# A third plain pair, a pool for the token sums, shifted weight parts and an in-place PV sum in a two-block transformer kernel

## The chip, the cores and the metric

The kernel runs on one core of a Trainium2 chip. The metric is the device time of one launch in microseconds. The kernel before takes 3598.26 us, the median of three runs (3597.29 to 3599.67).

## What is computed

Two transformer blocks of two layers each run one after the other on 512 tokens of width 1024, all in float32. The change lies mostly in the second block; each of its layers is

```python
h = rms_norm_2(x, norm1_g)
...
mix = jnp.concatenate([o_a.astype(x.dtype), o_b, o_c], axis=-1) @ w_out
x = x + mix
x = x + conv_glu_ffn(rms_norm_2(x, norm2_g), w_up, conv_w, conv_b, w_down)
```

with a causal convolution of width 3 over the tokens in the feed-forward:

```python
h = x @ w_up                       # 1024 x 5632
a, b = h[..., :D_FF], h[..., D_FF:]
...
return (jax.nn.silu(conv) * b) @ w_down
```

The first block has two attentions in parallel (eight heads of kind "a" and four of kind "b", over 768 keys in its first layer), an adaptive modulation computed from `c` and a gated branch sum; one part of the change touches the "a" heads there.

## The kernel before, in words

Every large product is made exact enough by splitting both operands into two parts: `hi` is the operand rounded to the short matmul format (`F32R`), `lo` the rest. A product is then three matmuls, hi by hi, hi by lo, lo by hi. All of them go through `mm` (L189). ACT makes the hi part of a weight tile by a cast (L291), DVE the lo part by a subtraction (L292); `whi` and `wlo` have two buffers each.

**The feed-forward of the second block** is `ffn2`. The 5632 columns of `w_up` come in 22 tiles of 256 columns: 11 pairs, one tile for the convolution branch and one for the gate branch. The first `NPLAIN` = 2 pairs are done by `plain`: 96 matmuls of 256 columns for a tile. The other 9 pairs are done by `strassen`, which needs only seven block products in place of eight: 7 x 12 = 84 matmuls of 256 columns. It takes sums of weight blocks (`strassen_weights`: POOL makes s3, s1, s2, s4 at L1818 to L1821, ACT and DVE split them into `shi` and `slo` at L1825 and L1826) and sums of token blocks. The seventh product, of s4, is owed: it is issued by `settle` in the course of the next tile, and s4 has two places in `shi` that are used in turn (`odd`).

The token sums are made once a layer, by the generator `steps` in `strassen_setup`, one of four steps after each plain tile: POOL multiplies x by the norm's `r` (L1768), ACT scales by the gain (L1769), POOL forms four differences (L1773 to L1776), ACT and DVE split the results into `ha`, `hb` and `ht` (L1778 to L1786). The plain tiles don't wait for `r`: they take x times the gain (`dhi`, `dlo`, `shi`, `slo` and `g`, L1756 and L1757, which use buffers that the block products and the down products need only later), and `r` is applied to their result (L1899, L1901).

The down products (`down`) run in chunks of two pairs: four of them, each 24 matmuls of 512 columns, are put behind the tiles of the next chunk, one behind each tile. Chunk 1 are the pairs 2 and 3.

All of these buffers but the weight parts and the scratch `tmp` are in the pool `fp`, which is opened when `ffn2` begins. The mixer's last product is cut in two halves of tokens; DVE adds each piece of it into x (L1727), ACT squares the sum (L367), the squares are summed (L369) and give `r` (L423 to L426).

**The "a" heads of the first block.** In `back` (L938 to L943) the upper 64 rows of a head's product with V are copied by ACT to a buffer `small`, and DVE adds them to the lower 64 rows. There are three such buffers, which also serve the sums of the modulation (`small<-raw,cc`, L592): these sums, their transposes (`n<-ident,small`) and the gate's product (`n<-h,whi`) are woven in between the heads.

The order on each engine is set when the program is built, by a scheduler that places an instruction where its inputs and its buffer are expected to be ready. A buffer that comes free earlier thus moves instructions.

## Time and profile before

| | |
|---|---|
| median of three runs | 3598.26 us |
| the profiled execution, its own time | 3594.57 us |
| its span, first to last instruction | 3592.8 us |
| mean granted TensorE clock | 0.979 |
| PE busy | 3394.7 us, 94% |
| DVE busy | 2526.9 us, 70% |
| ACT busy | 1497.2 us, 42% |
| POOL busy | 1053.7 us, 29% |

PE is TensorE, DVE is VectorE, ACT is ScalarE, POOL is GpSimd. The feed-forward of the second block runs from about 2533 to 2900 us in its first layer and from about 3203 to 3593 us in its second. The clock is a share of 2.4 GHz; 0.5 is the lower level of 1.2 GHz. A busy PE counts overlapping matmuls once, so its pace is read from the starts of the matmuls in the timeline.

### The profile page before, as it was taken

Reading aid. Unit: us, or ns where it says so; the run is one execution under the profiler, and the core shown is the slowest. Engines: PE = TensorE matmul, PEld = TensorE weight load, DVE = VectorE, ACT = ScalarE, POOL = GpSimd, SP = SyncE. Lnnn points to the kernel's source line nnn. Section 1 sums busy time; section 2 is a strip of 40 time slices with the busy share of each in tenths; the row PEclk is TensorE's granted clock in tenths of the full one; section 3 lists DMA queues with packets and bytes.
Section 4 is the critical chain, followed back from the end, with each engine's and each line's share of the span. In section 5 each row is a group of like instructions: output and inputs, shape, how many; then the busy total and the mean of one; then the engine's idle time right before and its main releaser. Section 6 shows DMA issues by size and latency. Waiting matters only on the chain.

```text
span 3592.8 us, 51031 instructions
## 1 busy us (share of the span) xinstructions
PE 3394.7 (94%) x19782; PEld 2936.4 (82%) x19782; DVE 2526.9 (70%) x4138; ACT 1497.2 (42%) x2415; POOL 1053.7 (29%) x968
## 2 busy tenths in 40 slices
PE   7998989999999999999999999979899998998998
PEld 5887878888888887877888887867899976778998
DVE  5558775558787765655767656797887769869775
ACT  4234545342222234355543334425544433455444
POOL 2232322320000012312231001563654326527441
PEclk9999999999999999999999999989999999999999
DMA  6376533412334423663444233443133342612331
GB/s 223 115 232 181 165 106 114 151 60 94 96 123 135 129 81 106 220 168 102 118 143 135 93 115 105 132 147 100 59 112 104 102 142 88 179 52 85 102 104 65
DMA packets 358609, 438.79 MB, mean 122 GB/s; under 512 B 41342, under 2 KB 310288, under 8 KB 358368
## 3 DMA queue, kind: packets, MB, share of 16 engines
q1 hardware_dynamic: 327648, 345.48, 32.0%
q0 software_dynamic: 19200, 71.17, 5.7%
q10 hardware_dynamic: 11520, 18.89, 1.6%
q8 instruction: 156, 2.56, 0.3%
q14 instruction: 85, 0.70, 0.1%
HBM read 363.78 MB, written 71.70 MB: 121 GB/s over the span
## 4 chain that ended last, share of the span: by engine, by line
PE 61%; DVE 10%; issue 3%; POOL 2%; ACT 2%; DMA 2%; ACTq 0%; SPq 0%; DVEq 0%; POOLq 0%
PE d L189 34%; PE s L189 18%; PE n L189 4%; DVE wlo L292 1%; PE o L189 1%; DVE sc L1424 1%; PE g L189 1%; DVE m L1423 1%; PE d L202 1%; PE b L202 1%; ACT whi L291 1%; DVE wlo L1813 0%; DVE slo L1826 0%; DVE hl L399 0%; DVE tmp L1355 0%
## 5 line engine op out<-in xcount | busy, mean ns | idle before, releaser
L189 PE MATMUL s<-h,whi 128*128 128x256 f32 (+3 forms) x2176 | 527.4, 335 | 11.1 <-ACT whi L291 6.4
L291 ACT CAST whi<-raw 128x2048 fp32r<-128x2048 f32 (+2 forms) x195 | 311.5, 1597 | 463.2 <-PE s L189 234.0
L292 DVE TENSOR_TENSOR wlo<-raw,whi 128x2048 fp32r<-128x2048 f32 (+3 forms) x179 | 357.5, 1997 | 180.1 <-ACT whi L291 179.2
L189 PE MATMUL d<-h,whi 128*128 128x512 f32 (+2 forms) x1456 | 443.7, 387 | 16.2 <-DVE h L1302 6.1
L189 PEld LDWEIGHTS s<-h,whi 128*128 128x128 f32 (+1 forms) x2176 | 373.9, 192 | 54.3 <-ACT whi L291 6.7
L189 PE MATMUL s<-h,wlo 128*128 128x256 f32 (+3 forms) x1088 | 360.9, 333 | 2.3 <-DVE wlo L292 2.3
L189 PEld LDWEIGHTS d<-h,whi 128*128 128x128 f32 (+1 forms) x1456 | 270.3, 191 | 76.2 <-DVE h L1302 8.3
L189 PE MATMUL d<-h,wlo 128*128 128x512 f32 (+2 forms) x728 | 278.3, 386 | 1.6 <-DVE wlo L292 1.6
L189 PEld LDWEIGHTS s<-h,wlo 128*128 128x128 f32 (+1 forms) x1088 | 207.8, 191 | 22.6 <-DVE wlo L292 3.0
L189 PE MATMUL n<-h,whi 128*128 128x512 f32 (+1 forms) x768 | 214.0, 363 | 4.4 <-ACT tmp L1006 2.8
L189 PE MATMUL d<-g,dhi 128*128 128x512 f32 x640 | 197.8, 391 | 0.0
L369 POOL TENSOR_TENSOR small<-small,tmp 128x256 f32<-128x256 f32 x36 | 32.8, 910 | 541.2 <-ACT tmp L367 510.8
L648 DVE TENSOR_REDUCE sm<-s 128x1 f32<-128x768 f32 (+1 forms) x160 | 134.2, 844 | 69.1 <-PE s L189 67.8
L650 ACT ACTIVATE e<-s,sm 128x768 f32<-128x768 f32 (+1 forms) x160 | 130.7, 818 | 116.7 <-DVE sm L648 96.0
L189 PE MATMUL s<-ku,ku 96*128 96x512 f32 (+3 forms) x720 | 154.6, 346 | 20.3 <-ACT e L650 14.4
L189 PE MATMUL d<-g,whi 128*128 128x256 f32 (+1 forms) x688 | 166.7, 337 | 6.4 <-DVE x L1101 2.3
L189 PE MATMUL s<-g,whi 128*128 128x256 f32 (+1 forms) x688 | 167.6, 335 | 0.0
L189 PEld LDWEIGHTS d<-h,wlo 128*128 128x128 f32 (+1 forms) x728 | 139.1, 191 | 29.5 <-issue 2.4
L189 PE MATMUL d<-ht,shi 128*128 128x256 f32 x864 | 161.4, 287 | 0.0
L189 PEld LDWEIGHTS s<-ku,ku 96*128 96x128 f32 (+1 forms) x720 | 120.8, 192 | 45.7 <-ACT e L650 20.4
L189 PEld LDWEIGHTS n<-h,whi 128*128 128x128 f32 x768 | 135.1, 192 | 23.8 <-ACT tmp L1006 3.7
L189 PE MATMUL d<-whi,h 128*128 128x256 f32 x768 | 148.8, 289 | 0.0
(553 smaller groups left out, 9000.9 us busy)
## 6 DMA issues: line engine op xcount, KB each, us to landing
raw<-in__w_up SPq DMA_DIRECT2D x88, 1024.0 KB, 5.1
raw<-in__w_in SPq DMA_DIRECT2D x53, 1024.0 KB, 5.4
araw<-in__w_ada SPq DMA_DIRECT2D x28, 1024.0 KB, 5.3
raw<-in__w_down SPq DMA_DIRECT2D x40, 512.0 KB, 3.5
draw<-in__w_down SPq DMA_DIRECT2D x40, 512.0 KB, 3.5
raw<-in__w_out SPq DMA_DIRECT2D x16, 1024.0 KB, 5.1
raw<-in__w_ada SPq DMA_DIRECT2D x15, 1024.0 KB, 9.7
U<-qd SPq DMA_DIRECT2D x32, 256.0 KB, 4.3
```

The source lines that it names most:

```text
L189: self.last = self.nc.tensor.matmul(*a, **k)
L202: return self.nc.tensor.transpose(*a, **k)
L291: self.nc.scalar.copy(hi, raw[:, 0:n])
L292: (self.nc.gpsimd if self.wpool else self.nc.vector).tensor_tensor(lo, raw[:, 0:n], hi.bitcast(F32), op=OP.subtract)
L369: (self.nc.gpsimd if e else self.nc.vector).tensor_tensor(acc[e], acc[e], sq, op=OP.add)
L648: nc.vector.tensor_reduce(m[:, 0:1], s, axis=AX.X, op=OP.max, negate=True)
L650: nc.scalar.activation(e, s, AF.Exp, bias=m[:, 0:1], accum_out=m[:, 1:2])
L1423: nc.vector.max(m8[t], sc[t])
L1424: nc.vector.match_replace(sc[t], m8[t], sc[t], TAKEN)
```

## The change

- `NPLAIN` goes from 2 to 3: the pair 2 is done by plain products as well, 192 matmuls in place of 168.
- Chunk 1's four down products all go behind the two tiles of pair 3, two behind each; `settle` follows each.
- `ha`, `hb` and `ht` get a pool of their own, `fq`, opened after `fp`. `fp` becomes smaller by them.
- In the first half of each step (k < 4), one DVE instruction multiplies x by the gain and by `r`, in place of POOL's multiply and ACT's scale.
- The parts of the weights of block products and of their sums lie one behind the other, 56 floats (224 bytes) into a slightly larger buffer. s4 has one place; `odd` is gone.
- In `back`, ACT copies one half of the product straight into `oa`, and DVE adds the other half in place; the buffer `small` isn't used.
- The last norm's small tiles get a tag of their own.

```diff
-NPLAIN = 2
+NPLAIN = 3
+SHIFT = 56
...
                 b = (hh % 2) * 64
-                tmp = self.small()[0:64]
-                nc.scalar.copy(tmp, po[64:128, 0:256])
-                nc.vector.tensor_tensor(oa[hh // 2][b:b + 64, q], po[0:64, 0:256], tmp, op=OP.add)
+                o = oa[hh // 2][b:b + 64, q]
+                nc.scalar.copy(o, po[64 - b:128 - b, 0:256])
+                nc.vector.tensor_tensor(o, po[b:b + 64, 0:256], o, op=OP.add)
                 return
...
-        self.shi = self.t(fp, [P, 5, 512], F32R, "shi", 1)
-        self.slo = self.t(fp, [P, 5, 512], F32R, "slo", 1)
+        self.shi, self.slo = [self.t(fp, [P, 2176], F32R, tag, 1)[:, SHIFT:SHIFT + 2048].rearrange("p (i n) -> p i n", i=4)
+                              for tag in ("shi", "slo")]
...
-        ha = [[self.t(fp, [P, H], F32R, "ha", 8) for _ in range(2)] for _ in range(4)]
-        hb = [[self.t(fp, [P, S], F32R, "hb", 8) for _ in range(2)] for _ in range(4)]
+        ha = [[self.t(fq, [P, H], F32R, "ha", 8) for _ in range(2)] for _ in range(4)]
+        hb = [[self.t(fq, [P, S], F32R, "hb", 8) for _ in range(2)] for _ in range(4)]
...
-        self.sT = [[self.t(fp, [P, 4, H], F32R, "ht", 8) for _ in range(2)] for _ in range(4)]
+        self.sT = [[self.t(fq, [P, 4, H], F32R, "ht", 8) for _ in range(2)] for _ in range(4)]
...
                     u.append(self.tmp(S))
+                    if k < 4:
+                        nc.vector.scalar_tensor_tensor(u[-1], x[k], gain[:, k:k + 1], r, op0=OP.mult, op1=OP.mult)
+                        continue
                     nc.gpsimd.tensor_tensor(u[-1], x[k], r, op=OP.mult)
                     nc.scalar.activation(u[-1], u[-1], AF.Copy, scale=gain[:, k:k + 1])
...
-        hi, lo = [self.t(self.wp, [P, 2048], F32R, tag, 2).rearrange("p (k n) -> p k n", k=KD) for tag in ("whi", "wlo")]
...
+        hi, lo = [self.t(self.wp, [P, 2048], F32R, tag, 2)[:, SHIFT:SHIFT + 1536].rearrange("p (i n) -> p i n", i=3)
+                  for tag in ("whi", "wlo")]
...
-        for d, v in ((slice(3, 5), flat(self.sraw)), (slice(1, 2), s2), (slice(2 - 2 * o, 3 - 2 * o), s4)):
+        for d, v in ((slice(2, 4), flat(self.sraw)), (slice(0, 1), s2), (slice(1, 2), s4)):
...
-            steps = self.strassen_setup(x, r, col["norm2"], fp)
+            steps = self.strassen_setup(x, r, col["norm2"], fp, self.pool(es, "fq", self.other()))
...
-                per = len(todo) // (2 * npair)
...
+                for i, t in enumerate(tiles):
+                    up(*t)
+                    if t[0] >= NPLAIN:
+                        for _ in range(len(todo) // (len(tiles) - i)):
```

In the built program the pool `fp` of the kernel before reaches over the place of the mixer's last operands (`mix`), which PE reads until its last matmul there; with `ha`, `hb` and `ht` outside it, `fp` ends below that place. So the order of instructions moves at the start of `ffn2`. First ACT, in the first layer of block 2, around the last pieces that the mixer adds into x. The squares are L367 before (L368 in the change), the plain parts L1756 (L1757). Before:

```order
L367 ACTIVATE tmp_22038<-x_21093 128x256
L367 ACTIVATE tmp_22041<-x_21094 128x256
L367 ACTIVATE tmp_22044<-x_21095 128x256
L367 ACTIVATE tmp_22123<-x_21090 128x256
L367 ACTIVATE tmp_22126<-x_21091 128x256
L367 ACTIVATE tmp_22129<-x_21092 128x256
L367 ACTIVATE tmp_22132<-x_21093 128x256
L367 ACTIVATE tmp_22135<-x_21094 128x256
L291 CAST whi_22369<-raw_22367 128x2048
L423 ACT_TABLE_LOAD
L423 ACTIVATE r_19222<-n_22048,sel_71 128x256
L1756 ACTIVATE dhi_22163<-x_21088,cols_2788_17499 128x256
L1756 ACTIVATE dhi_22163<-x_21089,cols_2788_17499 128x256
```

and in the change:

```order
L368 ACTIVATE small_21985<-x_21048 128x256
L1757 ACTIVATE dhi_22126<-x_21048,cols_2748_17459 128x256
L368 ACTIVATE small_21986<-x_21049 128x256
L1757 ACTIVATE dhi_22126<-x_21049,cols_2748_17459 128x256
L368 ACTIVATE tmp_21989<-x_21050 128x256
L1757 ACTIVATE dhi_22126<-x_21050,cols_2748_17459 128x256
L368 ACTIVATE tmp_21992<-x_21051 128x256
L1757 ACTIVATE dhi_22126<-x_21051,cols_2748_17459 128x256
L368 ACTIVATE tmp_21995<-x_21052 128x256
L1757 ACTIVATE shi_22124<-x_21052,cols_2748_17459 128x256
L368 ACTIVATE tmp_21998<-x_21053 128x256
```

Before, the first plain part `dhi` stands behind all squares of both token halves, a weight cast and the norm's first root. In the change each part stands right behind the square of the same x.

Next DVE, in the first layer, where the norm's `r` is ready and the token sums begin. L1899, L1888 and L1889 (L1905, L1894 and L1895 in the change) are the convolution of a plain tile, L1779 and L1782 (L1783 and L1786) the low parts of the sums. Before:

```order
L1899 TENSOR_TENSOR tmp_22329<-d_22231,r_19222 128x512
L1888 SCALAR_TENSOR_TENSOR ya_22331<-tmp_22329,colsw_2791_17509,ya_22331 128x511
L1899 TENSOR_TENSOR tmp_22337<-d_22232,r_19222 128x512
L1889 SCALAR_TENSOR_TENSOR ya_22331<-tmp_22329,colsw_2791_17509,ya_22331 128x510
L292 TENSOR_TENSOR wlo_22506<-raw_22503,whi_22505 128x2048
L1888 SCALAR_TENSOR_TENSOR ya_22339<-tmp_22337,colsw_2791_17509,ya_22339 128x511
L1779 TENSOR_TENSOR ha_22202<-tmp_22345,ha_22201 128x256
L1889 SCALAR_TENSOR_TENSOR ya_22339<-tmp_22337,colsw_2791_17509,ya_22339 128x510
L1779 TENSOR_TENSOR hb_22210<-tmp_22348,hb_22209 128x512
```

and in the change:

```order
L1905 TENSOR_TENSOR tmp_22292<-d_22194,r_19182 128x512
L1905 TENSOR_TENSOR tmp_22300<-d_22195,r_19182 128x512
L1770 SCALAR_TENSOR_TENSOR tmp_22308<-x_21048,cols_2748_17459,r_19182 128x512
L1894 SCALAR_TENSOR_TENSOR ya_22294<-tmp_22292,colsw_2751_17469,ya_22294 128x511
L1894 SCALAR_TENSOR_TENSOR ya_22302<-tmp_22300,colsw_2751_17469,ya_22302 128x511
L1895 SCALAR_TENSOR_TENSOR ya_22294<-tmp_22292,colsw_2751_17469,ya_22294 128x510
L1783 TENSOR_TENSOR ha_22165<-tmp_22308,ha_22164 128x256
L1895 SCALAR_TENSOR_TENSOR ya_22302<-tmp_22300,colsw_2751_17469,ya_22302 128x510
L1783 TENSOR_TENSOR hb_22173<-tmp_22310,hb_22172 128x512
L1770 SCALAR_TENSOR_TENSOR tmp_22443<-x_21049,cols_2748_17459,r_19182 128x512
```

The row L1770 is new: x times the gain times `r`, in place of POOL's L1768 for the same x.

Last PE, in the first layer of block 1, where the last "b" heads and the first "a" heads meet. `s<-tmp,sel` sums the squares of the "b" heads, `s<-ku,heads` spreads their norm, `s<-ku,ku` are scores, `n<-ident,small` the modulation's transposes, `n<-h,whi` the gate's product. Before:

```order
L189 MATMUL s_4035<-ku_4020,heads_75 128x512
L189 MATMUL s_4035<-ku_4020,heads_75 128x256
L189 MATMUL s_4047<-ku_3677,ku_3678 128x512 x3
L189 MATMUL s_4047<-ku_3677,ku_3678 128x256 x3
L189 MATMUL s_4060<-ku_3677,ku_3678 128x512 x3
L189 MATMUL s_4060<-ku_3677,ku_3678 128x256 x3
L202 MATMUL n_4162<-ident,small_4144 128x128 x2
L202 MATMUL n_4162<-ident,small_4145 128x128 x2
L189 MATMUL s_4116<-ku_3677,ku_3678 128x512 x3
L189 MATMUL s_4116<-ku_3677,ku_3678 128x256 x3
L189 MATMUL n_4170<-h_433,whi_3854 128x512
L189 MATMUL n_4170<-h_434,whi_3854 128x512
```

and in the change:

```order
L190 MATMUL s_3998<-tmp_3999,sel_71 8x512
L190 MATMUL s_3998<-tmp_3999,sel_71 8x256
L190 MATMUL s_3998<-tmp_4003,sel_71 8x512
L190 MATMUL s_3998<-tmp_4003,sel_71 8x256
L190 MATMUL s_3998<-tmp_4007,sel_71 8x512
L190 MATMUL s_3998<-tmp_4007,sel_71 8x256
L190 MATMUL n_4168<-h_433,whi_3854 128x512
L190 MATMUL n_4168<-h_434,whi_3854 128x512
L190 MATMUL n_4168<-h_433,wlo_3855 128x512
L190 MATMUL n_4168<-h_435,whi_3854 128x512
L190 MATMUL n_4168<-h_436,whi_3854 128x512
L190 MATMUL n_4168<-h_435,wlo_3855 128x512
```

Before, the gate's product comes after the spread norm and three groups of scores. In the change its 24 matmuls of 512 columns, and then 24 of 256, stand ahead of `s<-ku,heads`, among the last products of the heads with V.

## Rows read from the trace of the kernel before

**Rows 1.** The page: span, and busy time of each engine

```profile
span 3592.8 us, 51031 instructions
...
PE 3394.7 (94%) x19782; PEld 2936.4 (82%) x19782; DVE 2526.9 (70%) x4138; ACT 1497.2 (42%) x2415; POOL 1053.7 (29%) x968
```

**Rows 2.** Timeline of PE in the steady part: start us, us, instruction, xcount

```profile
2702.67 0.63 PE L189 MATMUL d<-g,dhi 128*128 128x512 f32 x2
...
2708.14 0.40 PE L189 MATMUL d<-hb,shi 128*128 128x256 f32 x2
...
2712.45 0.40 PE L189 MATMUL d<-ht,shi 128*128 128x256 f32 x2
```

**Rows 3.** Busy time by stretch, layer 0 of ffn2; count of instructions behind each

```profile
core 0: us, PE busy (x) PEld busy (x) DVE busy (x) ACT busy (x) POOL busy (x), PEclk, DMA share, GB/s
2525.00:2540.00 15.00, 11.08 (x80) 10.43 (x79) 11.48 (x27) 11.62 (x25) 3.20 (x4) 0.93 0.38 123
2560.00:2580.00 20.00, 20.00 (x169) 20.00 (x168) 19.19 (x17) 10.04 (x16) 19.92 (x15) 1.00 0.26 85
2580.00:2600.00 20.00, 12.02 (x82) 11.32 (x81) 19.93 (x17) 12.38 (x22) 17.23 (x12) 0.81 0.09 26
2600.00:2620.00 20.00, 18.53 (x120) 17.19 (x119) 19.81 (x22) 8.25 (x16) 14.16 (x10) 0.93 0.35 114
2700.00:2800.00 100.00, 100.00 (x690) 93.56 (x689) 79.21 (x110) 47.57 (x71) 46.49 (x27) 1.00 0.33 103
```

**Rows 4.** Busy time by stretch, layer 1 of ffn2

```profile
3200.00:3220.00 20.00, 13.95 (x86) 12.96 (x85) 14.82 (x29) 12.48 (x26) 8.06 (x5) 0.83 0.25 79
3260.00:3280.00 20.00, 11.85 (x58) 10.52 (x59) 20.00 (x17) 10.24 (x18) 20.00 (x14) 0.74 0.10 28
```

**Rows 5.** What PE waited for from 2520 to 2640: us, times, longest

```profile
PE d L189 <- ACT ha L1778: 4.4, 1, 4.4
PE d L189 <- ACT dhi L1756: 3.8, 1, 3.8
```

**Rows 6.** What PE waited for from 3200 to 3310

```profile
PE d L189 <- DVE ha L1779: 4.5, 2, 2.4
PE n L189 <- DVE small L369: 4.4, 1, 4.4
```

**Rows 7.** Timeline of POOL: its first work on the token sums, layer 0

```profile
2550.54 2.56 POOL L1768 TENSOR_TENSOR tmp<-x,r 128x512 f32<-128x512 f32 x2 [4.16 <-DVE r L426]
```

**Rows 8.** Timeline of PE: the first block product, layer 0

```profile
2586.20 0.40 PE L189 MATMUL d<-ha,whi 128*128 128x256 f32 x2
```

**Rows 9.** Groups of DVE instructions from 2555 to 2602, beside a busy POOL

```profile
L389 DVE TENSOR_TENSOR g<-ya,g 128x512 fp32r<-128x512 f32 x3 | 4.8, 1592 | 0.0
...
L1888 DVE SCALAR_TENSOR_TENSOR ya<-tmp,colsw,ya 128x511 f32<-128x511 f32 x3 | 3.8, 1250 | 0.0
...
L1779 DVE TENSOR_TENSOR ha<-tmp,ha 128x256 fp32r<-128x256 f32 x4 | 3.6, 892 | 0.7 <-ACT ha L1778 0.7
...
L1894 DVE TENSOR_TENSOR ya<-d,ya 128x512 f32<-128x512 f32 x4 | 2.7, 677 | 0.0
```

**Rows 10.** Groups of DVE instructions from 2640 to 2880, the steady part

```profile
L1888 DVE SCALAR_TENSOR_TENSOR ya<-tmp,colsw,ya 128x511 f32<-128x511 f32 x16 | 11.7, 750 | 3.4 <-ACT ya L1887 3.4
L389 DVE TENSOR_TENSOR g<-ya,g 128x512 fp32r<-128x512 f32 x15 | 9.7, 684 | 0.4 <-ACT g L388 0.4
```

**Rows 11.** Busy time from 450 to 475, between the two kinds of heads

```profile
450.00:475.00 25.00, 15.86 (x60) 11.04 (x61) 19.57 (x36) 10.11 (x16) 0.91 (x1) 0.73 0.28 82
```

**Rows 12.** What ACT waited for from 440 to 480

```profile
ACT tmp L953 <- DMA gb<-tmp: 5.1, 1, 5.1
```

**Rows 13.** Timeline of PE over the matmuls that read c, offset 32 bytes

```profile
131.42 0.63 PE L189 MATMUL s<-c,whi 128*128 128x512 f32 x2
...
133.51 0.39 PE L189 MATMUL s<-c,whi 128*128 128x256 f32 x2
...
134.56 0.59 PE L189 MATMUL n<-rn,ones 128*128 128x512 f32 x1
```

More of the change, by code (lines that the diff above doesn't have):

```diff
@@ L1731, in mixer2, with strassen_setup @@
         return x
-    def strassen_setup(self, x, r, gain, fp):
+    def strassen_setup(self, x, r, gain, fp, fq):
         nc = self.nc
         H = S // 2
-        self.fp, self.owed, self.odd = fp, None, 0
+        self.fp, self.owed = fp, None
         self.sraw = self.t(fp, [P, 2, 512], F32, "sraw", 1)
-        self.shi = self.t(fp, [P, 5, 512], F32R, "shi", 1)
-        self.slo = self.t(fp, [P, 5, 512], F32R, "slo", 1)
+        self.shi, self.slo = [self.t(fp, [P, 2176], F32R, tag, 1)[:, SHIFT:SHIFT + 2048].rearrange("p (i n) -> p i n", i=4)
+                              for tag in ("shi", "slo")]
         quarter = lambda t, i: t[:, i // 2, H * (i % 2):H * (i % 2) + H]
@@ L1749, in strassen_setup @@
             self.fB[0][1].append([both[:, 0:H], both[:, H:S]])
-            self.fB[1][0].append([quarter(t, 6 + k) for t in (self.shi, self.slo)])
-            self.fB[1][1].append([quarter(t, 2 + k) for t in (self.shi, self.slo)])
+            self.fB[1][0].append([quarter(t, 4 + k) for t in (self.shi, self.slo)])
+            self.fB[1][1].append([quarter(t, k) for t in (self.shi, self.slo)])
         for n in range(2):
@@ L1809, in strassen_weights @@
         blk = lambda t, i, j: t[:, 4 * j:4 * j + 4, P * i:P * i + P]
[L1810 to L1814 removed]
+        hi, lo = [self.t(self.wp, [P, 2048], F32R, tag, 2)[:, SHIFT:SHIFT + 1536].rearrange("p (i n) -> p i n", i=3)
+                  for tag in ("whi", "wlo")]
+        flat = lambda t: t.rearrange("p i (k n) -> p (i k) n", n=P)
+        for c, v in ((slice(0, 2), rv[:, :, 0:P]), (slice(2, 3), blk(rv, 1, 1))):
+            h_, l_ = flat(hi[:, c, :]), flat(lo[:, c, :])
+            nc.scalar.copy(h_, v)
+            nc.vector.tensor_tensor(l_, v, h_.bitcast(F32), op=OP.subtract)
         sv = lambda t, i: t[:, i, :].rearrange("p (k n) -> p k n", k=4)
@@ L1826, in strassen_weights @@
             nc.vector.tensor_tensor(sl, v, sh.bitcast(F32), op=OP.subtract)
-        s2, s4, s3, s1 = [[sv(t, i) for t in (self.shi, self.slo)] for i in (1, 2 - 2 * o, 3, 4)]
-        return {"a11": [blk(hi, 0, 0), blk(lo, 0, 0)], "a12": [blk(hi, 0, 1), blk(lo, 0, 1)], "a22": [blk(hi, 1, 1), blk(lo, 1, 1)],
-                "s3": s3, "s1": s1, "s2": s2, "s4": s4}
+        part = lambda ts, i: [sv(t, i) for t in ts]
+        w, ss = (hi, lo), (self.shi, self.slo)
+        return {"a11": part(w, 0), "a12": part(w, 1), "a22": part(w, 2),
+                "s2": part(ss, 0), "s4": part(ss, 1), "s3": part(ss, 2), "s1": part(ss, 3)}
     def block_product(self, ps, w, x, first=True):
@@ L1927, in ffn2 @@
             for npair in (2, 2, 2, 2, 2, 1):
-                per = len(todo) // (2 * npair)
-                for p0 in range(f0 // 2, f0 // 2 + npair):
-                    for c0, use, plain_use in ((p0 * 256, conv, scaled_conv), (F + p0 * 256, gate, gate)):
-                        up(p0, c0, use, plain_use)
-                        for _ in range(per):
+                tiles = [t for p0 in range(f0 // 2, f0 // 2 + npair)
+                         for t in ((p0, p0 * 256, conv, scaled_conv), (p0, F + p0 * 256, gate, gate))]
+                for i, t in enumerate(tiles):
+                    up(*t)
+                    if t[0] >= NPLAIN:
+                        for _ in range(len(todo) // (len(tiles) - i)):
                             todo.pop(0)()
                             self.settle()
-                todo = [lambda f=f0, g=g: down(f, g) for g in range(4)]
+                todo = todo + [lambda f=f0, g=g: down(f, g) for g in range(4)]
                 f0 += 2 * npair
@@ L2015, in after @@
                     self.mm(ps[:, t:t + 1], sq[:, t * P:(t + 1) * P], self.ones[:, 0:1], start=(i == 0), stop=(i == len(parts) - 1))
-            rs = self.tmp(4)
-            r, s_ = rs[:, 0:2], rs[:, 2:4]
+            r, s_ = [self.t(pool, [P, 2], F32, "rl", 4) for _ in range(2)]
             self.newton(r, s_, ps[:, 0:2], D, EPS)
```

5 lines of the change are left out of this document (removed).

## The prediction

> **What bounds the kernel now.** I read the page first: PE is busy 3394.7 of the 3592.8 us, DVE 70%, ACT and POOL far less [rows 1]. So time is won where PE stands still, or where its work gets shorter. The sum below is made against the profiled execution's own 3594.57 us, which is 3.7 us under the median of the runs (3598.26); I add that back at the end.
>
> Second, the timeline, for PE's pace. From 2702.67 to 2708.14 there are 24 matmuls of 512 columns: 0.228 us from start to start. The 36 of 256 columns up to 2712.45 take 0.120 us each [rows 2]. A count times these paces says how long a stretch should have taken.
>
> Third, the busy time by stretch in the second block's feed-forward. In its steady part PE is busy 100 of 100 us with DVE at 79 and ACT at 48 [rows 3]: nothing can be won there but by a shorter matmul. At its start and behind the plain tiles it is different:
>
> - Start, layer 0: 80 matmuls in 15 us, which at 0.120 are 9.6, so 5.4 lost [rows 3]. Layer 1: 86 in 20 us, 10.3, so 9.7 lost [rows 4]. Together 15. The clock is granted at 0.93 and 0.83 there: part of it is matmuls at the lower level after the idle time.
> - First block products, layer 0: 82 matmuls in 2580 to 2600 (9.8 us, 10.2 lost), and 120 in the next 20 us against 138 in the steady part (2.6 lost) [rows 3]. Layer 1: 58 in 20 us, 13.0 lost [rows 4]. Together 26; granted clock 0.81 and 0.74.
>
> Fourth, what PE waited for. At the start it is `dhi` in layer 0 (3.8 us) and the sum of squares `small` in layer 1 (4.4); at the first block products it is `ha`, from ACT and from DVE [rows 5, 6]. In that second stretch DVE is busy 19.9 of 20 us [rows 3, 4]. It is the engine that is late: not with one instruction, but with all that the token sums ask of it.
>
> **The change, part by part.**
>
> *Third plain pair.* Two tiles get 96 matmuls for 84, in two layers: 48 x 0.120 = +5.8 us, all on PE's path.
>
> *Start of the feed-forward.* `dhi` no longer waits for the mixer's last matmul, and the order puts each part behind the square of its x. The first tiles need only the first token half, complete 48 matmuls (5.8 us) before the mixer ends, and their weight parts are cast ahead of the mixer's end in both orders. What is late next is DVE: it now has an add and a low part for each piece that PE finishes, and PE finishes one in 6 x 0.120 = 0.72 us. The nearest row for a DVE instruction of this kind is 750 ns for 512 columns [rows 10], so about 0.4 for 256, twice per piece, 0.8 and a few sums of squares. DVE falls back by 2 us or so over the second half. I keep 2 us lost per layer, so 15 - 4 = -11. Bounds: 0 (DVE or the square sums take the whole wait over) and -15.
>
> *First block products.* The sums can begin when `r` is ready: POOL's first piece is at 2550.5 [rows 7], PE is through with the plain tiles at 2586.2 [rows 8], 35.7 us. With the start 5 us earlier and a third pair (192 x 0.120 = 23 us) the two times become about 2545.5 and 2604, 58.7 us. What has DVE to do in it? From the order, the instructions from L1905 to the parts of the first block product, counted at prices of the steady part (0.75 for a convolution step, 0.68 for a product or a low part of 512 columns [rows 10], half for 256, double for 1024), come to 42 us, an estimate; the four new products of x, gain and `r` are 3 of these. But DVE is slower beside POOL: 1250 ns for 750, 1592 for 684 [rows 9, 10]. Counted in the same way, the 47 us from 2555 to 2602 held 28 us of work, with POOL busy for some 41 of them (its share in [rows 3]): about 0.4 us lost per us of POOL. In the change POOL has some 46 us to do there (four products of 1.3 less, [rows 7], two more steps for the pair): 42 + 0.4 x 46 = 60 against 58.7. The last sums are ready some 10 us ahead of that, because the weight parts of the first block product are the end of the list. So the stall should shrink to the little that a list just about full leaves: I take 3 us per layer, 26 - 6 = -20. Bounds: -26 and 0.
>
> *Chunk 1's downs behind two tiles.* The same 4 x 24 matmuls, and PE has 48 of them per tile, 11 us, while DVE catches up. Nothing.
>
> *ACT's scale and POOL's product gone, four times a layer.* Both engines have idle time; the gain is in the sum above.
>
> *Weight parts at another offset.* 32 tiles x 84 = 2688 matmuls read weights that lie 224 bytes further. In the kernel before, nearly all matmul operands begin at the same place of a 512-byte line, by the built program; one exception are the weights of the products that read `c`, 32 bytes off. There nine matmuls of 256 columns take 1.05 us, 117 ns each, and nine of 512 take 2.09, 232 ns [rows 13], against 120 and 228 [rows 2]. The block products have 256 columns, so the nearest row is 117: 2688 x -0.003 = -8 us. Bounds: -8 ns, nearly three times what that row shows (-21), and +1 ns (+3), since its 512-column matmuls were slower by 4. Another offset need not act like 32 bytes. The Trainium skill, "SBUF — State Buffer", section "SBUF: two separate sides", says that PE's ports never wait on anyone; by that an offset is worth nothing, and the sum would be 8 us higher. No aligned and shifted pair of the same product stands in this trace.
>
> *One place for s4.* Its cast by ACT must now wait until PE has done the s4 product of the tile before. It is the last of a tile's casts in ACT's order, and s4 is needed only in the course of the next tile. Cover: ACT is idle 52 of 100 us [rows 3], 8 us of a tile's 84 x 0.120 + 24 x 0.228 = 15.6. Nothing; what it costs without cover is a rival.
>
> *PV halves in place.* The same ACT and DVE instructions on the same shapes: nothing by itself. But `small` is no longer taken, and the gate's product moves up into a stretch where PE is busy 15.9 of 25 us at a clock of 0.73 [rows 11], partly because ACT waited 5.1 us for a buffer that a DMA was emptying [rows 12]. 24 matmuls of 512 and 24 of 256 are 8.3 us that can fill the 9 us of idle time. The modulation's sums on DVE must then be done earlier too, and DVE is busy 19.6 of 25 there. I take -5; bounds 0 and -8.
>
> *Order elsewhere.* The scheduler moves small things in both mixers. I see no direction: 0, with 5 us either way.
>
> Sum: +5.8 - 11 - 20 - 8 - 5 = -38.2. 3594.6 - 38.2 = 3556.4, plus 3.7: **3560 us**.
>
> **The rivals.**
>
> *The head stall stays (A).* DVE and POOL hold each other up more than my 0.4, so that the longer list of DVE takes its full contended price: 42 us x 47/28 = 70 against 58.7, 11 us late per layer instead of 3. Then 3560 + 16 = 3576; with a delay that also meets the clock's lower level, up to 3580. For it: that factor is measured, and the four new products have both inputs in SBUF. Against: POOL has less to do per us of this longer stretch. The Trainium skill, "SBUF — State Buffer", in the same section, says that a DVE instruction with two SBUF inputs and a GpSimd instruction that reads SBUF exclude each other for the whole of an instruction. By that, moving work from POOL to DVE frees nothing, since both stand in one queue; the time is that of this rival. The trace agrees in part: instructions that read `d`, not SBUF alone, keep 677 ns there [rows 9].
>
> *The shift is worth its bound (B).* 13 us more than my 8: 3547.
>
> *The start isn't freed (C).* The parts are early in the order, but DVE or the sum of squares, on which layer 1 waited already [rows 6], takes over the wait. The change then doesn't do there what the order says: 3571.
>
> *ACT blocks on s4 (D), slower.* With one place, ACT stands in front of the cast until PE has issued the owed product, and behind it in ACT's queue are the copies of the next tile's results and the next weight casts. This decides from 8 us of waiting a tile, ACT's spare time. Each us beyond costs 32 us, once a tile. At 2 us beyond: 3560 + 64 = 3624, slower. Against: at 48% busy, and with the owed product in the first half of a tile, the wait should be about half a tile or less.
>
> **How the numbers follow.** My forecast with its own bounds has 0.52, A 0.22, B 0.10, C 0.08, D 0.08. Below 3547 lies half of B, above 3586 lie D and a part of A's worst: the range is **3540 to 3586**. A measurement of this kernel can tell about 0.2% from no change, 7.2 us. Forecast, B and C lie wholly on the faster side, A nearly so: faster 0.86. The same needs A with the upper bounds of the other terms, or D just begun: 0.06. Slower is D: 0.08.
>
> **What would show it.** Start right: PE goes from the mixer's products to the plain tiles within 2 us, the clock stays near 1. Head right: the tile behind the plain tiles takes about 84 x 0.120 + 48 x 0.228 = 21 us with its two downs, with no wait for `ha` above 2 us; if A holds, DVE is still at 19.9 of 20 there. Shift right: 36 matmuls of a block product take 4.2 us, not 4.31. D: ACT's casts of `shi` wait longer for PE, and PE waits in the steady part. Wrong altogether if PE's busy time in the steady part falls under 100%.

## The result and the profile after

The change is faster: 3558.16 us median of four runs (3554.81 to 3564.70) beside 3598.97 us of the kernel before in the same job (four runs, 3597.29 to 3602.52). The ratio is 0.989, 95% interval 0.9874 to 0.9905. The profiled execution took 3554.81 us, against 3594.57 before; its granted clock is 0.982, against 0.979.

The page of the kernel after answers to [rows 1]:

```profile
span 3553.0 us, 51094 instructions
...
PE 3381.7 (95%) x19830; PEld 2926.0 (82%) x19830; DVE 2505.1 (71%) x4114; ACT 1478.5 (42%) x2383; POOL 1028.9 (29%) x948
```

PE's busy time fell by 13.0 us, the span by 39.8. So most of what was won is time in which PE stood still. Where it was won is to be read from the starts of a few matmuls in the timelines of the two kernels, in us:

| | before | after | won so far |
|---|---|---|---|
| first `s<-oh,whi` (first block, behind the heads) | 628.72 | 610.35 | 18.4 |
| end of the first block | 2227.28 | 2204.76 | 22.5 |
| last `d<-mix` of the second block, layer 0 | 2532.98 | 2514.00 | 19.0 |
| last down matmul, layer 0 | 2891.09 | 2863.47 | 27.6 |
| last `d<-mix`, layer 1 | 3202.38 | 3178.91 | 23.5 |
| last down matmul, layer 1 | 3563.09 | 3524.28 | 38.8 |

About half of the gain lies at one place in the first block, before 628 us. The two feed-forwards of the second block are worth 8.6 and 15.3, 24 together. The mixers ahead of them gave back 3.5 and 4.1.

Each column is one execution. Nine of the kernels below (all but e1 to e3) have the order of the kernel after, on PE, DVE, ACT, POOL and in the DMA issues, up to the last mixer matmul of layer 0; in these ten traces the first `s<-oh,whi` comes between 610.35 and 615.55 and that mixer matmul between 2514.00 and 2520.38, and the kernel after is the earliest in both. So differences of a few us in this table are not the change's for sure. Steadier is the time from the first `o<-PT,V` to the first `s<-oh,whi`, the end of the heads of the first layer: 169.1 to 170.7 us in these ten and in e1 below, 186.7 before and 188.2 in e3. By that this place is worth 16 to 19 us.

The busy time by stretch, kernel after (columns: stretch, its length, busy time and count of PE, PEld, DVE, ACT, POOL, then the granted clock, the DMA share and GB/s):

```profile
450.00:475.00 25.00, 23.24 (x117) 18.32 (x116) 22.47 (x37) 10.59 (x15) 5.66 (x2) 0.86 0.71 189
475.00:520.00 45.00, 45.00 (x306) 41.38 (x305) 24.81 (x53) 26.17 (x56) 16.93 (x17) 1.00 0.40 108
2505.00:2520.00 15.00, 15.00 (x125) 14.89 (x124) 13.98 (x32) 12.63 (x30) 3.33 (x4) 1.00 0.23 73
2560.00:2580.00 20.00, 16.72 (x131) 16.32 (x130) 16.42 (x17) 8.21 (x14) 18.17 (x13) 0.95 0.27 85
2580.00:2600.00 20.00, 17.03 (x137) 16.63 (x136) 17.68 (x19) 11.53 (x17) 10.13 (x7) 0.97 0.15 48
2600.00:2620.00 20.00, 19.34 (x117) 16.97 (x116) 18.18 (x24) 7.92 (x12) 9.02 (x5) 1.00 0.42 132
2700.00:2800.00 100.00, 99.21 (x704) 92.84 (x703) 82.40 (x113) 45.95 (x71) 42.60 (x24) 1.00 0.34 109
```

The first row answers to [rows 11]: PE is busy 23.24 of 25 us where it was 15.86. The start of the feed-forward (third row) has no gap and a clock of 1.00, where [rows 3] showed 0.93. The stretch with the first block products, 10.2 us short in [rows 3], is short by less than 4 (137 matmuls are 16.4 of its 20 us). But the steady part, 100 of 100 us in [rows 3], is at 99.21: PE waits now where it did not before.

In numbers: for each feed-forward I took the time between matmul starts and subtracted the count of matmuls times their pace (0.120 us for 256 columns, 0.2275 for 512; for shifted block products the pace measured below). What is left is lost time, in us, both layers together, from one execution of each kernel. In before and e1, whose feed-forwards are alike, the lost time agrees to 0.3 us. "Start and plain" goes from the last mixer matmul to the first `ha`; "length" is the whole stretch.

| kernel | start and plain | first 60 us of block products | the rest | lost | length |
|---|---|---|---|---|---|
| before | 16.3 | 28.6 | 0.3 | 45.1 | 718.8 |
| after | 9.6 | 9.1 | 4.5 | 23.2 | 694.8 |
| e1_pv_only | | | | 45.4 | |
| e3_fq_only | 1.2 | 32.6 | 0.6 | 34.5 | 708.9 |
| e4_shift0 | 11.2 | 6.7 | 0.9 | 18.8 | 699.0 |
| e5_two_pairs | 0.4 | 29.4 | 20.5 | 50.4 | 715.2 |
| e6_pool_mult | 12.6 | 8.8 | 11.7 | 33.1 | 704.7 |
| e8_dve_all | 5.0 | 12.5 | 9.1 | 26.6 | 698.2 |
| e9_shift8 | 10.6 | 8.2 | 8.5 | 27.3 | 702.5 |
| e10_s4_apart | 9.8 | 6.8 | 0.5 | 17.0 | 688.7 |
| e11_s4_dve_all | 5.0 | 10.6 | 0.6 | 16.2 | 687.8 |
| e12_s4_four_pairs | 7.0 | 7.5 | 2.1 | 16.5 | 695.0 |
| e13_s4_two_pairs | 0.4 | 29.1 | 0.5 | 30.0 | 694.7 |

The start itself is gone. The timeline of PE after shows the mixer's last product and the first plain one 0.12 us apart, the plain pace:

```profile
2514.00 0.28 PE L190 MATMUL d<-mix,wlo 128*128 128x256 f32 x1
2514.12 0.28 PE L190 MATMUL d<-dhi,whi 128*128 128x256 f32 x1
```

What "start and plain" still loses, 5.4 and 4.2 us, is a new stall inside the third plain pair, the matmuls at the lower clock right behind it included. The longest waits of PE from 2500 to 2620 us (columns: engine and line, what it waited for, us in total, times, longest):

```profile
PE d L190 <- DVE wlo L293: 2.1, 1, 2.1
PE d L190 <- ACT tmp L1860: 1.9, 1, 1.9
PE d L190 <- ACT whi L292: 1.1, 1, 1.1
```

ACT's timeline shows why the third pair's weight cast is late: in front of it in ACT's order stand the casts of the token sums, and those wait for POOL.

```profile
2571.75 0.62 ACT L1785 CAST ht<-tmp 128x512 fp32r<-128x512 f32 x1 [1.51 <-POOL tmp L1778]
2572.27 1.90 ACT L292 CAST whi<-raw 128x2048 fp32r<-128x2048 f32 x1
```

PE waits for this `whi` until 2574.22 and then for its `wlo` until 2576.85. The wait for `tmp` comes later, among the block products. No wait for `ha` is left among them, which were the longest of [rows 5, 6].

### The profile page after: what moved, and what is told of

It is laid out like the page before. It is cut to its first block, busy times and chain, and to the rows that moved or that the text cites. A ratio compares the mean times of both kernels' runs of the same rounds, so it can differ in the third digit from the quotient of the medians.

```text
span 3553.0 us, 51094 instructions
## 1 busy us (share of the span) xinstructions
PE 3381.7 (95%) x19830; PEld 2926.0 (82%) x19830; DVE 2505.1 (71%) x4114; ACT 1478.5 (42%) x2383; POOL 1028.9 (29%) x948
## 5 line engine op out<-in xcount | busy, mean ns | idle before, releaser
L292 ACT CAST whi<-raw 128x2048 fp32r<-128x2048 f32 (+3 forms) x199 | 319.0, 1603 | 452.0 <-PE s L190 224.4
L190 PE MATMUL d<-g,whi 128*128 128x256 f32 (+1 forms) x752 | 178.2, 331 | 6.9 <-DVE x L1102 2.3
L190 PEld LDWEIGHTS d<-h,wlo 128*128 128x128 f32 (+1 forms) x728 | 139.2, 191 | 29.1 <-DVE wlo L293 2.7
L190 PEld LDWEIGHTS s<-ku,ku 96*128 96x128 f32 (+1 forms) x720 | 119.9, 189 | 41.0 <-ACT e L651 19.2
L190 PEld LDWEIGHTS d<-g,whi 128*128 128x128 f32 x752 | 127.1, 189 | 22.8 <-issue 4.0
```

Source lines behind the costliest of these rows:

```text
L190: self.last = self.nc.tensor.matmul(*a, **k)
L292: self.nc.scalar.copy(hi, raw[:, 0:n])
```

## The experiments

### The first block: PV halves in place

**e1_pv_only**: the kernel before with only this part.

```diff
-tmp = self.small()[0:64]
-nc.scalar.copy(tmp, po[64:128, 0:256])
-nc.vector.tensor_tensor(oa[hh // 2][b:b + 64, q], po[0:64, 0:256], tmp, op=OP.add)
+o = oa[hh // 2][b:b + 64, q]
+nc.scalar.copy(o, po[64 - b:128 - b, 0:256])
+nc.vector.tensor_tensor(o, po[b:b + 64, 0:256], o, op=OP.add)
```

> The kernel before with the PV halves added in place and nothing else of the change. Theory S (the mixer's gain comes from PV leaving the shared buffer `small`): the heads of the first block's first layer shrink as in the changed kernel, about 18 us between the first s<-tmp,sel and the first s<-oh,whi, and the time is about 3599 - 20 = 3579. Rival R1 (my prediction's split: 5 us here, the rest of the 40 in the second block): 3594. Rival R2 (the mixer moved for another reason, with which PV has nothing to do): 3599.

Measured: 3576.01 us, ratio 0.9943 [0.9924, 0.9962]; its profiled span is 3574.0, 18.8 less than before. This one edit gives nearly half of the whole gain. The first product behind the heads, in the timelines of before, after and e1:

```profile
628.72 0.71 PE L189 MATMUL s<-oh,whi 128*128 128x512 f32 x2
```
```profile
610.35 0.70 PE L190 MATMUL s<-oh,whi 128*128 128x512 f32 x2
```
```profile
610.49 0.71 PE L189 MATMUL s<-oh,whi 128*128 128x512 f32 x2
```

e1 is where the change is, to 0.14 us, and its feed-forward loses what it lost before (45.4). What moved is the chain to the gate's product. First DVE's sums 21 and 22 of the 26 of the modulation, before (both in one row) and in e1 (there sum 22 follows at 423.95), then SP's last load of `w_ada`, before and after, and the gate's product behind these, before and after:

```profile
457.94 0.59 DVE L590 TENSOR_SCALAR small<-raw,cc 128x256 f32<-128x256 f32 x2
```
```profile
420.88 0.38 DVE L590 TENSOR_SCALAR small<-raw,cc 128x256 f32<-128x256 f32 x1
```
```profile
470.26 0.39 SPq L564 DMA_DIRECT2D raw<-in__w_ada  x1
```
```profile
435.77 6.38 SPq L565 DMA_DIRECT2D raw<-in__w_ada  x2
```
```profile
474.67 0.63 PE L189 MATMUL n<-h,whi 128*128 128x512 f32 x2
```
```profile
447.35 0.73 PE L190 MATMUL n<-h,whi 128*128 128x512 f32 x2
```

The sums run 37 us earlier, the load 28 us earlier (it is the second of the two issues in the last SP row, and ends at 442.15), the gate's product 27 us earlier, and PE has it where it stood still. Before, sum 20 runs at 421.22 and sum 21 only behind the first PV addition, which frees a `small` at 452.80; in e1 it follows sum 20 by 1.8 us. It is not this product alone: between 450 and 520 us seven of the gate's groups of 24 matmuls begin after, and four before. PE also keeps its clock better: 0.86 and 1.00 in the two stretches of the table after, 0.73 [rows 11] and 0.96 before. The second stretch of before:

```profile
475.00:520.00 45.00, 40.35 (x252) 35.48 (x251) 35.90 (x76) 20.61 (x43) 13.57 (x12) 0.96 0.39 100
```

In the 70 us PE starts 419 matmuls where it started 310.

**e2_pv_own_buffer**: PV as before, but its copy in a buffer of its own, so that it no longer shares `small`; the room for it came from `small` (3 buffers to 2).

```diff
-tmp = self.small()[0:64]
+tmp = self.t(self.sp, [P, SEG], F32, "pv", 1)[0:64]
-NSM = 3
+NSM = 2
```

> The kernel before, PV still through a copy and not in place, but the copy in a buffer of its own (one), and `small` with two buffers in place of three. The order puts the gate's product ahead of s<-ku,heads here as well. Theory S (sharing is what cost): most of e1's gain, 3579 to 3588, less what one buffer fewer for the other uses of `small` costs. Rival (adding in place is what pays, since it saves the wait for the copy's buffer or shortens PV's own chain): 3599 or slower.

Measured: 3618.80 us, 1.0061 [1.0044, 1.0078], slower. The gate's product moved ahead here too, but the gap only moved with it, to 475 to 490 us:

```profile
450.00:475.00 25.00, 22.39 (x99) 14.25 (x99) 20.97 (x43) 9.97 (x13) 4.74 (x1) 1.00 0.52 161
475.00:490.00 15.00, 9.36 (x46) 7.42 (x47) 12.23 (x16) 3.94 (x5) 4.51 (x1) 0.77 0.96 271
```

From the first `o<-PT,V` to the first `s<-oh` it takes 190.5 us, against 186.7 before and 169.2 in e1. This run changes two things (the sharing and the number of buffers), and does not tell them apart. That the in-place addition is the cause is shown by e1. That it works by the shared `small` is argued from the order of the rows (sums 21 and 22 come only behind the addition of a PV copy, and ahead of it where there is none in `small`), and no run shows it by itself.

### The feed-forward: pool, pairs, and who makes the sums

**e3_fq_only**: the kernel before with `ha`, `hb`, `ht` in the pool `fq`.

```diff
-        ha = [[self.t(fp, [P, H], F32R, "ha", 8) for _ in range(2)] for _ in range(4)]
+        ha = [[self.t(fq, [P, H], F32R, "ha", 8) for _ in range(2)] for _ in range(4)]
...
-            steps = self.strassen_setup(x, r, col["norm2"], fp)
+            steps = self.strassen_setup(x, r, col["norm2"], fp, self.pool(es, "fq", self.other()))
```

> The kernel before with ha, hb and ht in a pool of their own, opened after the other. Theory: the start of the second block's feed-forward loses 16 us in the kernel before (6.7 and 9.7) and under 1 us in this one; the stall at the first block products stays, since DVE's list there is the same and only begins earlier together with PE: about 3599 - 15 = 3584. Rival: what is won at the start is lost at the first block products, because DVE, not PE, sets when these can run, and its list begins no earlier: 3595 to 3599.

Measured: 3583.11 us, 0.9966 [0.9952, 0.9979]. The start's loss falls from 16.3 to 1.2 us, nearly the whole of it, by the pool alone. The first block products lose a little more (32.6 for 28.6), since PE now reaches them sooner and the sums are no earlier. The feed-forwards are 9.9 us shorter.

e1 and e3 also show from where the mixers' loss comes. From the end of the first block to the last mixer matmul of layer 0 it takes 305.7 us before, 308.9 in e1, 305.0 in e3 and 309.2 after: this part comes with the PV edit. From the last down matmul of layer 0 to the last mixer matmul of layer 1, e1 takes as long as before, e3 4.7 us longer: this part comes with the pool. Why is not shown.

**e5_two_pairs**: the change with `NPLAIN = 2`.

```diff
-NPLAIN = 3
+NPLAIN = 2
```

> The changed kernel with two plain pairs in place of three. My prediction's theory: the third pair gives DVE 23 us and so takes most of the stall at the first block products away; without it the stall of 14 us a layer is back, 28 against the 18 that the changed kernel still loses there and in its third pair, less 5.8 for the matmuls saved: about 3558 + 4 = 3562, and 3558 + 14 = 3572 if the stall grows as I had predicted it to shrink. Rival (what is left over when the PV edit, the new pool and the shift are taken from the 40 us is only 2 us or so, so the third pair does nothing): 3556 to 3560.

Measured: 3577.96 us, 0.9944 [0.9928, 0.9961]; the third pair is worth 20 us in the change, and the intervals are apart. But the table says that only a part of that lies in the head, the plain part and the first 60 us of block products. There the loss is 29.4 without the third pair and, counting the plain part with it (0.4 to 9.6), the pair saves 11 us for 5.8 of added matmuls. The other 16 are in the steady part (20.5 for 4.5). That part begins 60 us behind the first block product, which needs the token sums. The waits of ACT from 2650 to 2850 us, after and e5:

```profile
ACT whi L1819 <- DMA raw<-in__w_up: 26.6, 10, 4.4
```
```profile
ACT whi L1819 <- DMA raw<-in__w_up: 36.0, 12, 4.9
```

ACT waits for the weight load itself. Before has no such row in this stretch. Next follow the DMA issues on SP, before and after (one tile takes 15.3 to 15.6 us), each followed by ACT's cast of the second load shown:

```profile
2757.36 0.37 SPq L296 DMA_DIRECT2D draw<-in__w_down  x1
2765.06 0.37 SPq L296 DMA_DIRECT2D raw<-in__w_up  x1
2772.66 0.37 SPq L296 DMA_DIRECT2D draw<-in__w_down  x1
```
```profile
2780.45 1.57 ACT L1812 CAST whi<-raw 128x1024 fp32r<-128x1024 f32 x2 [0.52 <-PE d L189]
```
```profile
2731.91 0.37 SPq L297 DMA_DIRECT2D draw<-in__w_down  x1
2732.85 0.37 SPq L297 DMA_DIRECT2D raw<-in__w_up  x1
2747.27 0.37 SPq L297 DMA_DIRECT2D draw<-in__w_down  x1
2748.98 0.37 SPq L297 DMA_DIRECT2D raw<-in__w_up  x1
```
```profile
2740.76 1.57 ACT L1819 CAST whi<-raw 128x1024 fp32r<-128x1024 f32 x2 [4.43 <-DMA raw<-in__w_up]
```

Before, loads for the up and the down products take turns, 7.7 us apart. After, the up load goes out 0.9 us behind a down load. The cast of `whi` that needs the load of 2732.85 runs at 2740.76, 7.9 us later, having waited 4.43 for it. Before, the load of 2765.06 is cast at 2780.45, 15.4 us later, with no wait for it. What came in between: s4 is summed over its own place in `raw`, and with one place in `shi` its cast stands behind PE's s4 product, in the next tile. Until then this `raw` buffer can take no new load. ACT's cast of s4 and DVE's low part of it, after:

```profile
2727.81 0.62 ACT L1830 CAST shi<-raw 128x512 fp32r<-128x512 f32 x1 [0.52 <-PE d L190]
```
```profile
2732.14 0.68 DVE L1831 TENSOR_TENSOR slo<-raw,shi 128x512 fp32r<-128x512 f32 x1
```

The low part ends at 2732.82, and the load goes out at 2732.85. The next group tests that.

### s4: one place

**e10_s4_apart**: the change, with the sum s4 in a small buffer of its own in place of `raw`.

```diff
-        nc.gpsimd.tensor_tensor(s4, s2, blk(rv, 0, 1), op=OP.add)
+        d4 = self.t(self.fp, [P, 512], F32, "s4raw", 1).rearrange("p (k n) -> p k n", k=4)
+        nc.gpsimd.tensor_tensor(d4, s2, blk(rv, 0, 1), op=OP.add)
...
-        for d, v in ((slice(2, 4), flat(self.sraw)), (slice(0, 1), s2), (slice(1, 2), s4)):
+        for d, v in ((slice(2, 4), flat(self.sraw)), (slice(0, 1), s2), (slice(1, 2), d4)):
```

> The changed kernel with POOL's sum s4 in a tile of its own, not written over the raw weights, so that the raw buffer is free before ACT has cast s4. Theory Q (the single place of s4 delays the raw buffer, and with it the next weight load, which now stands behind a down load on its queue; ACT waits for it at 10 of 11 tiles, and PE loses 3.4 and 0.8 us in the steady part): ACT's casts no longer wait for a load, the steady part loses under 1 us, 3558 - 3 = 3555. Rival (with matmuls of 117 ns DVE's share is just too high and the steady part loses this anyway): 3558.

**e13_s4_two_pairs**: the same with two plain pairs.

```diff
-NPLAIN = 3
+NPLAIN = 2
```

> As e10, with two plain pairs. With two pairs and s4 over the raw weights the kernel took 3578, and of the 27 us that PE lost more than with three pairs 16 lay in the steady part. Theory Q: these 16 go, 3562, and the third pair is worth some 7 us. Rival (the steady loss is DVE, which is still behind from the start): 3575 to 3578, and the third pair is worth 20.

Measured: e10 3555.23 us, 0.9887 [0.9872, 0.9902]; e13 3556.14, 0.9890 [0.9874, 0.9907]. SP in e10 is back to turns:

```profile
2733.77 0.37 SPq L297 DMA_DIRECT2D draw<-in__w_down  x1
2741.61 0.37 SPq L297 DMA_DIRECT2D raw<-in__w_up  x1
```

and the stretch from 2650 to 2850 us is full again. The rows are of before, after, e5, e10 and e13:

```profile
2650.00:2850.00 200.00, 200.00 (x1389) 187.57 (x1389) 160.20 (x222) 95.62 (x143) 91.40 (x52) 1.00 0.33 103
```
```profile
2650.00:2850.00 200.00, 198.14 (x1392) 184.65 (x1391) 159.79 (x215) 92.03 (x139) 78.79 (x45) 1.00 0.34 107
```
```profile
2650.00:2850.00 200.00, 194.51 (x1352) 180.35 (x1351) 158.50 (x213) 89.97 (x138) 85.18 (x48) 1.00 0.31 100
```
```profile
2650.00:2850.00 200.00, 200.00 (x1397) 186.50 (x1396) 164.56 (x221) 95.11 (x141) 83.24 (x48) 1.00 0.32 106
```
```profile
2650.00:2850.00 200.00, 200.00 (x1409) 187.04 (x1408) 161.82 (x218) 94.19 (x140) 80.27 (x47) 1.00 0.32 105
```

So the hold on `raw` is the cause: with s4 beside it the loss is gone, with three pairs and with two. With two pairs it costs 20 us (e5 0.9944 against e13 0.9890, intervals apart; 20.5 lost against 0.5). With three it costs 4 in the feed-forward (4.5 against 0.5), and in the total nothing that the intervals can tell (e10 against after). Why it costs so much more with two is not shown. e10's feed-forwards are 6.1 us shorter than those of after, but its last mixer matmul of layer 0 comes at 2520.4 in place of 2514.0. The edit does not touch that part, and the order of instructions up to there is the same on every engine: the 6.4 us lie between two executions, and hide the gain.

The group also says what the third pair is worth by itself. The totals with s4 apart, 3555.23 against 3556.14, can't tell it from none. By the stretches e10 and e13 lose 9.8 + 6.8 against 0.4 + 29.1 in the head, 13 us for 6.8 of matmuls (48 x 0.120, and 336 x 0.003 for tiles that lose the shift), and the feed-forwards are 6.0 us shorter with it (688.7 against 694.7). In the two profiled executions this gain is hidden, since e13's last mixer matmul of layer 0 comes at 2514.8, 5.5 us ahead of e10's; the totals' intervals, some 5 us to either side, leave room for it.

**e12_s4_four_pairs**: e10 with `NPLAIN = 4`.

```diff
-NPLAIN = 3
+NPLAIN = 4
```

> As e10, with four plain pairs. Theory: the fourth pair costs 5.6 us (48 matmuls at 117) and can only win back the 9 us that the first block products still lose in both layers, while the 10 of the plain tiles stay: between 3551 and 3556. Rival (the stall only moves on behind the fourth pair, or the down products of the first chunk, which now all wait for the next chunk, bring a new one): 3560 or more.

Measured: 3554.83 us, 0.9887 [0.9872, 0.9902]: no change in the total. The head still loses 14.5 us, for the plain tiles have their own stall on `whi` and `wlo` (1.2 and 2.4 us in layer 0). The feed-forwards are 6.3 us longer than e10's, and the mixers ahead of them 5.3 shorter in this execution.

### POOL or DVE for the token products

**e6_pool_mult**: the change, with POOL's multiply and ACT's scale for all eight.

```diff
-                    if k < 4:
-                        nc.vector.scalar_tensor_tensor(u[-1], x[k], gain[:, k:k + 1], r, op0=OP.mult, op1=OP.mult)
-                        continue
```

> The changed kernel with POOL's product and ACT's scale for all eight pieces, as before. Theory P (in the changed kernel POOL's chain is what is late: ACT stands for POOL's differences before it casts the third pair's weights, and DVE has idle time there): four products of 1.3 to 1.7 us more on POOL, a stall larger by 3 to 6 us a layer, 3564 to 3570. Rival D (DVE's list is what is late, as I predicted): DVE has four instructions fewer, the stall shrinks by up to 3 us a layer, 3552 to 3558. By the rule that DVE and GpSimd exclude each other it makes little difference: 3558.

**e8_dve_all**: the change, with all eight on DVE.

```diff
-                    if k < 4:
-                        nc.vector.scalar_tensor_tensor(u[-1], x[k], gain[:, k:k + 1], r, op0=OP.mult, op1=OP.mult)
-                        continue
-                    nc.gpsimd.tensor_tensor(u[-1], x[k], r, op=OP.mult)
-                    nc.scalar.activation(u[-1], u[-1], AF.Copy, scale=gain[:, k:k + 1])
+                    nc.vector.scalar_tensor_tensor(u[-1], x[k], gain[:, k:k + 1], r, op0=OP.mult, op1=OP.mult)
```

> The changed kernel with the product of x, gain and r on DVE for all eight pieces: no product on POOL, no scale on ACT. Theory P (POOL's chain is late): a stall smaller by 2 to 5 us a layer, 3549 to 3554. Rival D (DVE's list is late): larger by 2 to 3 us a layer, 3562 to 3564.

**e11_s4_dve_all**: e8's edit on top of e10.

```diff
+        d4 = self.t(self.fp, [P, 512], F32, "s4raw", 1).rearrange("p (k n) -> p k n", k=4)
+        nc.gpsimd.tensor_tensor(d4, s2, blk(rv, 0, 1), op=OP.add)
...
+                    nc.vector.scalar_tensor_tensor(u[-1], x[k], gain[:, k:k + 1], r, op0=OP.mult, op1=OP.mult)
```

> As e10, and all eight products of x, gain and r on DVE. With them the third pair and the start lost 4.9 in place of 9.6 us and the first block products 12.6 in place of 9.2, but the steady part lost 8.9 in place of 4.2. Theory Q: the steady loss goes, and what stays is a gain of 1 or 2 on e10: 3553. Rival: the steady loss comes from DVE's longer list, which runs on into the first tiles, and stays: 3559.

Measured: e6 3567.37 us, 0.9913 [0.9897, 0.9930]; e8 3559.39, 0.9896 [0.9881, 0.9910]; e11 3554.28, 0.9887 [0.9873, 0.9902]. In the table, with none, four and eight products on DVE the plain part loses 12.6, 9.6 and 5.0, and the reason, argued and not shown, is that ACT waits less for POOL ahead of the weight casts. The first block products lose 8.8, 9.1 and 12.5. What PE waits for there in layer 0 is ACT's copy `tmp` (1.9 us) in all three and DVE's `slo` (0.5, 1.1 and 1.2); with eight on DVE a wait for ACT's `shi` is added (1.1). Four to eight (after to e8, e10 to e11) is worth nothing that can be told, and the head's two columns together are 18.7 and 17.5. None to four is 21.4 to 18.7 in the head; e6's 9 us in the total are mostly its steady part (11.7 for 4.5), where ACT waits 27.9 us for the weight load from 2650 to 2850; the intervals of e6 and after overlap. e8's steady part loses 9.1, and with s4 apart (e11) 0.6.

### The shift

**e4_shift0** and **e9_shift8**: the change with the weight parts not shifted, and shifted by 32 bytes.

```diff
-SHIFT = 56
+SHIFT = 0
```

> The changed kernel with SHIFT = 0: the weight parts of the block products at the start of their buffers. Theory: the 2688 matmuls take 120 ns again in place of 117, which is 8 us: 3558 + 8 = 3566, and no wait in the steady part, so that the single place of s4 is seen to cost nothing. Rival by the rule that PE's ports wait on no one: the pace doesn't change with the offset, 3558. Rival (s4's single place costs): PE still waits in the steady part, 3 us in the two layers together, as with the shift.

```diff
-SHIFT = 56
+SHIFT = 8
```

> The changed kernel with the shift of 8 floats, 32 bytes, in place of 224. Theory: what counts is that the weights and the tokens no longer begin at the same place of a 512-byte line; 32 bytes do as well, as the matmuls that read c show: 117 ns, 3558. Rival: the size of the offset matters, and 32 bytes give another pace: 120 ns and 3563 to 3566.

Measured: e4 3563.14 us, 0.9909 [0.9893, 0.9926]; e9 3563.19, 0.9907 [0.9892, 0.9922]. Both medians are 5 us above the change, and both intervals overlap with its. The paces can be told. Start of the 36 matmuls of three block products and the next one behind them, shifted by 224 bytes, not at all, by 32 bytes:

```profile
2680.29 0.40 PE L190 MATMUL d<-hb,shi 128*128 128x256 f32 x2
...
2684.49 0.40 PE L190 MATMUL d<-ht,shi 128*128 128x256 f32 x2
```
```profile
2681.17 0.40 PE L190 MATMUL d<-hb,shi 128*128 128x256 f32 x2
...
2685.48 0.40 PE L190 MATMUL d<-ht,shi 128*128 128x256 f32 x2
```
```profile
2684.30 0.40 PE L190 MATMUL d<-hb,shi 128*128 128x256 f32 x2
...
2688.55 0.40 PE L190 MATMUL d<-ht,shi 128*128 128x256 f32 x2
```

These are 4.20, 4.31 and 4.25 us: 116.7, 119.7 and 118.1 ns for one matmul. The edits change nothing but where the weights lie. All traces agree: over some 2,000 matmuls of block products in the steady parts the mean is 116.7 or 116.8 ns in the eight kernels with 224 bytes, 119.9 in the five with none, two layouts of the weights among these, and 118.3 in e9. By pace the shift is worth 2688 x 3.0 ns = 8.1 us against e4. But the feed-forward is shorter by 4.2 only (699.0 and 694.8): e4's steady part loses 0.9, that of after 4.5. That the late weight load is hidden at 15.6 us a tile and not at 15.3 is a guess; e9, with a pace between the two, loses 8.5. So e9's total says little of 32 bytes: of the 12.0 us by which its execution is longer than that of after, in the same order of instructions, 3.3 are there at the last mixer matmul of layer 0, and 7.7 lie in the feed-forwards, 4.0 of these in the steady loss.

## Why the prediction was right, and where its terms were not

The forecast of 3560 is 2 us from the median, and no rival's time came in. By its terms it was less exact than that, because errors cancel. Against the sum of -38.2:

- **Third plain pair, +5.8**: as worked out, in matmuls. What it bought is in the next two terms; for the pair alone it is 13 us, by e10 and e13.
- **Start of the feed-forward, -11**: the start is gone entirely (PE 0.12 us behind the mixer), better than the 2 us a layer that I kept for DVE. But the plain tiles now lose 9.6 in the third pair, on ACT's casts behind POOL's sums, which the prediction did not have at all. Net -6.7, inside the bounds. Rival C, the start not freed, is refuted by e3: the pool alone takes the loss there from 16.3 to 1.2.
- **First block products, -20**: measured 28.6 to 9.1, -19.5. The size is right, to half a us, and partly by luck: the 0.4 us of DVE lost per us of POOL is 0.46 by the prediction's own numbers, (47 - 28) / 41, which gives a list of 63 us for its 60, and a part of the stall moved ahead into the third pair. Rival A, the longer list of DVE at the fully contended price, would have left 22 there. The Trainium skill, "SBUF — State Buffer", section "SBUF: two separate sides", has a DVE instruction with two SBUF inputs and a GpSimd instruction that reads SBUF exclude each other; the prediction's reading, that moving work from POOL to DVE frees nothing, is not borne out in full: moving four products from POOL to DVE did not lengthen the head (21.4 us to 18.7), though moving four more moved the loss from one place to another (18.7 and 17.5).
- **Shift, -8**: measured by pace 3.0 ns a matmul, 8.1. The nearest row [rows 13] had the size, in part by luck: at that row's own offset, 32 bytes, the block products take 118.1 ns (e9), which is half of the gain. Rival B, the bound, is out. The same section of the Trainium skill says that PE never waits on anyone; read as the prediction read it, that an offset is worth nothing, this does not agree with 119.7 ns and 116.7 ns for the same products. About half of these 8 us is not in the feed-forward's length (699.0 to 694.8): the steady part lost 3.6 more.
- **PV halves and the gate's product, -5**: the term that was mis-sized. It is worth -18.4 at the first `s<-oh` (16 to 19 by the steadier measure) and -18.8 alone in e1, outside of the bound of -8 that I gave. I had counted one gate's product of 24 and 24 matmuls that fills the idle time of one window, 450 to 475 us. What failed is that choice of the window: the gap continues to 520 us (PE busy 40.35 of 45 us before, 45.00 after), it was partly at the lower clock, and the whole chain of DVE sums, load and product moved up by 27 to 37 us, with the gate's products that follow.
- **One place for s4, 0**: wrong in mechanism, small in size. The cover that I named, ACT's idle time, is there: ACT's own casts of `shi` wait for PE no longer than before (7.1 us from 2650 to 2850, 24.1 before). What I left out is that s4 is summed over `raw`, so that the late cast holds a buffer which a DMA is to fill. It costs 4 us of the feed-forward with three pairs, 20 with two. Rival D had the cause, one place, and placed the wait at ACT's queue; it came at SP's. The prediction's own last test, PE under 100% in the steady part, is met in small: 99.21.
- **Order elsewhere, 0 with 5 either way**: the mixers of the second block gave back 7.6 us (3.5 ahead of layer 0, 4.1 ahead of layer 1), more than the 5 that I allowed. By e1 and e3 the first part comes with the PV edit and the second with the pool; I had given neither a side effect.

So: in these two executions the first block gained 13 to 17 us more than forecast (18.4 behind the heads, 22.5 at its end), the feed-forward 9 less (24.0 for 33.2), and the mixers gave back 7.6. The total was right by more than its parts deserved.

## What to carry to other kernels

Before a buffer is made single, look for every buffer that the delayed instruction reads, and above all for one that a DMA must refill: the wait shows up not where the instruction stands but at the load queue. The rows to read are the DMA issues on SP and the time from a load's issue to its first cast (15.4 us before, 7.9 after). And measure a multi-part change by its parts: here one edit in the first block gave half, and the third plain pair, worth 20 us in the change as it stands, is worth 6 us of the feed-forward once s4 is out of `raw`, and nothing that the totals can tell.

## What was not expected of the hardware

A matmul of 128 by 256 takes 116.7, 118.1 or 119.7 ns from start to start in otherwise equal programs, by where its weights lie (shifted by 224, by 32 or by 0 bytes). Over the 2688 matmuls that is 8.1 us of 3558, and the totals can't tell it: e4 is 5 us slower by its median, with intervals that overlap.

The same instructions in the same order end at other times from one execution to the next: the kernels after, e4 and e9 have one order on all engines and in the DMA issues, and their last mixer matmul of layer 0 comes at 2514.0, 2514.1 and 2517.3; e10, with the same order up to there, has it at 2520.4. This sets a limit to what totals can say here; the lost time of a stretch says more.
